# The sample block's state-space states: one product over 128 tokens per four sequences, for pairs of 32-row strips

## The chip, the core and the metric

The kernel runs on one core of one Trainium2 chip. The metric is device microseconds (us) of one execution of the whole program; the time of a version is the median of its runs. The engines are named as the profile names them: PE (TensorE matmuls) and PEld (its weight loads), DVE (VectorE), ACT (ScalarE), POOL (GpSimd) and SP (which issues the DMAs). PEclk is the clock that the throttle granted to TensorE, as a share of full speed.

## The reference, cut to what matters

One inference step of a layer: 1,024 prompt tokens of one new stream and 16 new tokens for each of 8 running streams (128 "sample" tokens) go through three token mixers side by side (stick-breaking attention, a Mamba-2 state-space group called SSD, forgetting attention called FoX), then a cross-attention and a feed-forward block. The change touches one product of the SSD group: the new state of each running stream.

```python
# sample group: b = 8 sequences, one chunk of 16 tokens each; 8 heads of 64 (p), state size 128 (n), 2 B/C groups
a_cum = jnp.cumsum(a, axis=2)
to_end = jnp.exp(a_cum[:, :, -1:, :] - a_cum)
chunk_states = jnp.einsum('bcshn,bcsh,bcshp->bchpn', B, to_end, x)   # sum over the 16 tokens s
chunk_decay = jnp.exp(a_cum[:, :, -1, :])
h_final = chunk_decay * h0 + chunk_states                             # output s_ssm, (8, 8, 64, 128)
```

## The kernel before, in words

All 1,152 tokens are nine blocks of 128; block 8 holds the sample tokens, sequence b in rows 16b to 16b+15. The first part of the program computes the input projections and, woven into one another by Python generators, three streams of work: the prompt attention (lines 560 to 606), the attention of the running streams over their caches (lines 863 to 959, cache rows loaded by SP at lines 882 and 942) and the SSD generator `ssd_gen` (lines 960 to 1200). The second part (output projection, cross-attention, feed-forward) is dense matmuls.

`ssd_gen` works through the blocks in the order 8, 0, 1, ..., 7. A block has the steps `load` (SP, lines 1037 to 1041), `prepare` (PE transposes at lines 1054 and 1058, POOL scalings through line 1030), `weights` (the masked decay matrix), `states`, `outputs` (eight products at line 1156) and `write`. A prompt block carries its state in `hT` (lines 1094 and 1100). Block 8 takes the `else` branch of `states`: the old states of four sequences lie in one SBUF tile of 128 x 3072 (`st8[hf]`, hf = 0 and 1, the first 2,048 columns), as 4 sequences b times 4 pairs of heads j times 128 states, with the pair's 2 x 64 channels on the partitions. For each half hf the branch

- transposes the old states (line 1129) and multiplies them with C for the token outputs: strips that are 32 columns of the array wide, accumulated in the PSUM tile `yo` (line 1132);
- makes the new states. `xe` holds x times its decay to the end of the chunk (128 tokens x 512 channels), `Bn` holds B (128 tokens x 2 groups x 128). A 32-row strip of tokens has two sequences. POOL first masks `Bn` by the parity of the sequence within its strip (line 1118, one 128 x 256 product for each of the two groups); a matmul over one strip (line 1139) then gives the states of its two sequences side by side in 256 columns. The two strips of a half go to two PSUM tiles, one of pool `psd` (2 buffers, one of them `yo` during this branch) and one of `pst` (3 buffers), and their matmuls are put to the scheduler as one group (`together`);
- decays and adds on DVE, one 128 x 128 operation for each sequence and pair of heads (line 1144), 32 in all, and stores the half (SP, line 1146).

Inputs of these matmuls are plain float32. The trace holds two matmul records for each of them and one for a transpose.

No order is written out by hand around this place. The kernel is recorded through a framework that sorts each engine's instructions at build time by a timeline of its own, with the priorities that the code gives (`hp`, `together`), and then inserts the waits. Every engine runs its list in that order. So a changed instruction can move others. Tiles of a pool are handed on when their last reader is done.

Of the kernel before, what the change touches and what calls it, by code (L numbers as in the profile page):

```python
# [12 lines left out]
ALU = mybir.AluOpType  # L13
# [4 lines left out]
P = 128  # L18
# [44 lines left out]
def tile_hybrid_step(ctx: ExitStack, tc: tile.TileContext, a: dict):  # L63
    nc = tc.nc
    ACT, DVE, POOL, PE, SP = nc.scalar, nc.vector, nc.gpsimd, nc.tensor, nc.sync
# [44 lines left out]
    def pd():  # L110
        return ps_t(psd, "d")
# [4 lines left out]
    def pT():  # L116
        return ps_t(pst, "t")
# [23 lines left out]
    rows = xc_t()  # L141
# [825 lines left out]
    def ssd_gen():  # L967
# [3 lines left out]
        bmask = sc[:, 1536:1544]  # L971
# [116 lines left out]
        def states(i, A, B, t1):  # L1088
            xT, br, zt, Bn, cb, xn, xd, xe, xD = views(A, B)
            hs = slice(8 * i, 8 * i + 8)  # L1090
            if i < 8:
                ps = pd()
                for g in range(2):
                    PE.matmul(ps[:, g * 256:(g + 1) * 256], xT[:, 6 + g, :], hT[:, g * 256:(g + 1) * 256],
                              start=True, stop=True)
                DVE.tensor_tensor(out=h3(t1), in0=h3(ps), in1=bc(ea[:, hs]), op=ALU.mult)
                heads_tt(hT, hT, dec[:, hs])
                ps = pd()
                for g in range(2):
                    PE.matmul(ps[:, g * 256:(g + 1) * 256], Bn[:, g * P:(g + 1) * P], xe[:, g * 256:(g + 1) * 256],  # L1100
                              start=True, stop=True)
                DVE.tensor_tensor(out=hT, in0=hT, in1=ps, op=ALU.add)
            else:
                hs_, cps = [], []
                for g, t in enumerate(st8):
                    hst = t[:, :2048].rearrange("p (u n) -> p u n", n=P)

                    cp = t[:, 2048:2304]
                    POOL.memset(cp, 0.0)
                    cv = bass.AP(cp.tensor, cp.offset, [list(cp.ap[0]), [64, 4], [48, 2], [1, 16]])  # L1110
                    POOL.tensor_copy(cv, xT[:, 6 + g, :].rearrange("p (i e t) -> p i e t", e=2, t=DEC_S))
                    hs_.append(hst.rearrange("p (b j) n -> p b j n", j=4))
                    cps.append(cp)
                yo = pd()
                bms = []
                for g in range(2):
                    bm = (A, B)[g][:, 2560:2816]
                    POOL.tensor_tensor(out=bm.rearrange("p (e n) -> p e n", n=P),
                                       in0=Bn[:, g * P:(g + 1) * P].unsqueeze(1).to_broadcast([P, 2, P]),
                                       in1=maskh.unsqueeze(2).to_broadcast([P, 2, P]), op=ALU.mult)  # L1120
                    bms.append(bm)
                for hf in range(2):
                    hst = hs_[hf]
                    for e in range(2):
                        h0 = []
                        for b in (e, 2 + e):
                            tp = pT()
                            for j in range(4):
                                PE.transpose(tp[:, j * P:(j + 1) * P], hst[:, b, j, :], ident)
                            h0.append(sg_t())  # L1130
                            ACT.copy(h0[-1], tp)
                        together([lambda r=32 * (2 * hf + x), g=g, x=x: PE.matmul(
                            yo[r:r + 32, g * 256:(g + 1) * 256], cps[g][:, 2 * r + 32 * e:2 * r + 32 * e + 32],
                            h0[x][:, g * 256:(g + 1) * 256], start=e == 0 and g == 0, stop=e == 1, skip_group_check=True)
                            for g in range(2) for x in (1, 0)])
                        yield
                    for j in range(4):
                        pss_ = [pd(), pT()]
                        together([lambda r=32 * (2 * hf + x), x=x: PE.matmul(
                            pss_[x][:, :256], xe[r:r + 32, j * P:(j + 1) * P], bms[j // 2][r:r + 32, :],  # L1140
                            start=True, stop=True) for x in range(2)])
                        for b in range(4):
                            bb = 4 * hf + b
                            DVE.scalar_tensor_tensor(hst[:, b, j, :], hst[:, b, j, :], dcol[:, 8 * j + bb:8 * j + bb + 1],
                                                     pss_[b // 2][:, b % 2 * P:(b % 2 + 1) * P], ALU.mult, ALU.add)
                    SP.dma_start(out=a["s_ssm"][0, 4 * hf:4 * hf + 4].rearrange("b h p n -> (b h p) n")
                                 .rearrange("(u p) n -> p u n", p=P), in_=hst.rearrange("p b j n -> p (b j) n"))
                    yield
                DVE.tensor_tensor(out=h3(t1), in0=h3(yo), in1=bc(ea[:, hs]), op=ALU.mult)
            pool_tt(t1, t1, xD, ALU.add)  # L1150
# [915 lines left out]
```

## Time and profile before

| | us |
|---|---|
| Median of 3 runs | 1885.78 |
| Lowest and highest of them | 1882.77, 1887.08 |
| The profiled execution's own time | 1894.55 |
| Its span in the trace | 1892.8 |

Positions are given in us from the start of the profiled execution's span. The branch for block 8 lies at 537.6 to 573.3 in it (first transpose of line 1129, last operation of line 1144). The mean granted TensorE clock over the span is 0.988.

### The profile page before, as it was taken

The numbers are of one execution on the slowest core, as the hardware profiler recorded it, in microseconds if no ns is written. First come the engines' busy times: TensorE is split into PE (matmuls) and PEld (weight loads), VectorE is DVE, ScalarE is ACT, GpSimd is POOL, SyncE is SP. The second block draws the span as 40 slices with busy tenths as digits, with TensorE's granted clock in tenths as the row PEclk, the third lists the DMA queues.
The fourth block names the chain that finished last, engine by engine and source line by source line (L and its number), as shares of the span: only waits on it lengthen the run. The fifth ranks groups of instructions, "written<-read, shape, count | busy, mean of one in ns | idle before, by whom it ended". The sixth has DMA issues, their size and how long they took to land.

```text
span 1892.8 us, 32368 instructions
## 1 busy us (share of the span) xinstructions
PE 1837.7 (97%) x12136; PEld 1638.6 (87%) x12136; DVE 886.4 (47%) x1798; ACT 802.1 (42%) x1719; POOL 617.9 (33%) x921
## 2 busy tenths in 40 slices
PE   7999999999999989999999989999999999999998
PEld 5899778888967767899988889999999999888886
DVE  3412323475656863444444586333333333455554
ACT  6522544545455862344332374333333333344443
POOL 7622425445115673111112107444444542000000
PEclk9999999999989999999999999999999999999999
DMA  9465654437587883245576124233322223657572
GB/s 338 145 189 149 206 142 133 147 109 207 179 249 228 282 290 102 108 134 173 173 271 219 56 81 112 75 87 79 76 71 70 70 70 105 207 187 243 174 243 89
DMA packets 291068, 296.64 MB, mean 157 GB/s; under 512 B 80092, under 2 KB 242884, under 8 KB 290912
## 3 DMA queue, kind: packets, MB, share of 16 engines
q1 hardware_dynamic: 290912, 294.57, 49.6%
q8 instruction: 96, 1.57, 0.3%
q14 instruction: 60, 0.49, 0.1%
HBM read 225.12 MB, written 69.91 MB: 156 GB/s over the span
## 4 chain that ended last, share of the span: by engine, by line
PE 83%; DMA 5%; DVE 4%; POOL 3%; ACT 3%; issue 2%; SPq 0%; DVEq 0%; POOLq 0%; ACTq 0%
PE psd L1868 11%; PE psd L328 10%; PE psd L329 10%; PE psd L330 10%; PE pst L1868 8%; PE pss L1868 4%; PE pss L328 3%; PE pss L330 3%; PE pss L329 3%; PE pso L1868 2%; POOL wl L132 2%; PE pst L328 1%; PE pst L329 1%; PE pst L330 1%; PE pso L593 1%
## 5 line engine op out<-in xcount | busy, mean ns | idle before, releaser
L132 POOL TENSOR_TENSOR wl<-wr,wh 128x256 fp32r<-128x256 f32 (+2 forms) x184 | 142.1, 805 | 233.0 <-ACT wh L292 232.8
L328 PE MATMUL psd<-act,wh 128*128 128x384 f32 x528 | 182.3, 345 | 0.0
L330 PE MATMUL psd<-act,wl 128*128 128x384 f32 x528 | 181.1, 343 | 0.6 <-POOL wl L132 0.6
L329 PE MATMUL psd<-act,wh 128*128 128x384 f32 x528 | 181.7, 344 | 0.0
L1868 PE MATMUL pst<-bT,tr 128*128 128x256 f32 (+1 forms) x1068 | 155.0, 293 | 0.0
L1868 PEld LDWEIGHTS pst<-bT,tr 128*128 128x128 f32 x1068 | 144.9, 188 | 0.1
L330 PE MATMUL psd<-wh,act 128*128 128x512 f32 (+3 forms) x424 | 136.9, 324 | 0.0
L329 PE MATMUL psd<-wl,act 128*128 128x256 f32 (+3 forms) x414 | 134.2, 325 | 2.7 <-POOL wl L132 2.7
L328 PE MATMUL psd<-wh,act 128*128 128x256 f32 (+3 forms) x414 | 133.3, 326 | 1.4 <-DMA act<-osc 1.0
L1868 PE MATMUL psd<-bT,tr 128*128 128x320 f32 (+1 forms) x912 | 132.8, 295 | 0.7 <-POOL tr L132 0.7
L1868 PEld LDWEIGHTS psd<-bT,tr 128*128 128x128 f32 x912 | 124.7, 188 | 1.0 <-POOL tr L132 0.9
L132 POOL TENSOR_TENSOR tr<-u,tr 128x256 fp32r<-128x256 f32 x110 | 82.6, 779 | 101.7 <-ACT tr L1704 83.8
L253 POOL TENSOR_SCALAR sm<-sm 128x1 f32<-128x1 f32 (+2 forms) x27 | 9.1, 338 | 297.3 <-ACT y L1970 207.8
L1843 DVE TENSOR_TENSOR tr<-tr,pst 128x256 f32<-128x256 f32 (+1 forms) x86 | 38.6, 449 | 139.9 <-ACT tr L1840 106.6
L330 PEld LDWEIGHTS psd<-act,wl 128*128 128x128 f32 x528 | 99.2, 188 | 3.2 <-issue 1.9
L132 POOL TENSOR_TENSOR ws<-ws 128x256 f32<-128x256 f32 (+2 forms) x100 | 69.3, 721 | 98.1 <-DVE ws L522 83.9
L328 PEld LDWEIGHTS psd<-act,wh 128*128 128x128 f32 x528 | 99.4, 188 | 2.2 <-issue 1.8
L329 PEld LDWEIGHTS psd<-act,wh 128*128 128x128 f32 x528 | 99.3, 188 | 1.9 <-issue 1.5
L132 POOL TENSOR_TENSOR tr<-raw,tr 128x256 fp32r<-128x256 f32 x94 | 69.2, 765 | 83.9 <-ACT tr L1704 75.7
L1704 ACT CAST tr<-tr 128x384 fp32r<-128x384 f32 (+1 forms) x70 | 37.6, 538 | 123.0 <-DMA tr<-hidsc 117.3
L329 PEld LDWEIGHTS psd<-wl,act 128*128 128x128 f32 x414 | 79.2, 191 | 10.9 <-POOL wl L132 4.0
L292 ACT CAST wh<-wr 128x512 fp32r<-128x512 f32 (+2 forms) x90 | 52.5, 622 | 81.7 <-PE psd L330 32.0
(643 smaller groups left out, 4730.5 us busy)
## 6 DMA issues: line engine op xcount, KB each, us to landing
u<-w_down SPq DMA_DIRECT2D x40, 512.0 KB
raw<-w_down SPq DMA_DIRECT2D x26, 512.0 KB
st<-qksc SPq DMA_DIRECT2D x48, 256.0 KB
wr<-w_in SPq DMA_DIRECT2D x44, 256.0 KB
tr<-hidsc SPq DMA_DIRECT2D x57, 192.0 KB
hidsc<-tr SPq DMA_DIRECT2D x34, 288.0 KB
qksc<-sg SPq DMA_DIRECT2D x48, 192.0 KB
wr<-cache_sb_k SPq DMA_DIRECT2D x32, 256.0 KB
```

What stands on the lines that cost most here:

```text
L132: POOL.tensor_tensor(out=out[:, a0:a1], in0=in0[:, a0:a1], in1=in1[:, a0:a1], op=op)
L253: POOL.tensor_scalar(v, ss, inv, EPS, ALU.mult, ALU.add)
L292: ACT.copy(hi, raw)
L328: PE.matmul(out, ah, bh, start=start, stop=False)
L329: PE.matmul(out, ah, bl, start=False, stop=False)
L330: PE.matmul(out, al, bh, start=False, stop=stop)
L593: return PE.matmul(po[r:r + 64, q_], vt[:, 2 * (k0 + i) + j, :], pfs[i][:, sl], start=start and k0 == 0 and (j == 0 or qp > 0), stop=k0 + ...
L1704: ACT.copy(hi, src)
L1843: DVE.tensor_tensor(out=at(out, g), in0=at(x, g), in1=ps[g][:, :GW[g]], op=op)
L1868: PE.matmul(dst[g][:, :GW[g]], x[:, ka], y[:, k, :], start=start and k == 0 and m == 0, stop=stop and k == 3 and m == 2, skip_group_check= ...
```

## The change

For each half, POOL now masks `Bn` with `bmask`, the one-hot map from token to sequence, into four blocks of 128 columns: tokens of other sequences become zeros. One matmul over all 128 tokens then gives the states of the four sequences of a half, for one pair of heads, in 512 columns. There are 8 such matmuls in place of 16 strips, 4 POOL products of 128 x 512 in place of 2 of 128 x 256, and one PSUM tile for each matmul, by turns of `psd` and `pst`. The masked rows lie in free columns of the same SBUF tiles (A, B and the two of `st8`). The DVE operations, the transposes and the stores are the same. Line numbers after this place are smaller by one.

```diff
-                bms = []
-                for g in range(2):
-                    bm = (A, B)[g][:, 2560:2816]
-                    POOL.tensor_tensor(out=bm.rearrange("p (e n) -> p e n", n=P),
-                                       in0=Bn[:, g * P:(g + 1) * P].unsqueeze(1).to_broadcast([P, 2, P]),
-                                       in1=maskh.unsqueeze(2).to_broadcast([P, 2, P]), op=ALU.mult)
-                    bms.append(bm)
+                rows = [[], []]
+                for hf in range(2):
+                    for g, t in enumerate((A, B)):
+                        bm = (t, st8[g])[hf][:, (2560, 2304)[hf]:(3072, 2816)[hf]]
+                        POOL.tensor_tensor(out=bm.rearrange("p (b n) -> p b n", n=P),
+                                           in0=Bn[:, g * P:(g + 1) * P].unsqueeze(1).to_broadcast([P, 4, P]),
+                                           in1=bmask[:, 4 * hf:4 * hf + 4].unsqueeze(2).to_broadcast([P, 4, P]), op=ALU.mult)
+                        rows[hf].append(bm)
...
                     for j in range(4):
-                        pss_ = [pd(), pT()]
-                        together([lambda r=32 * (2 * hf + x), x=x: PE.matmul(
-                            pss_[x][:, :256], xe[r:r + 32, j * P:(j + 1) * P], bms[j // 2][r:r + 32, :],
-                            start=True, stop=True) for x in range(2)])
+                        ps = (pd, pT)[j % 2]()
+                        PE.matmul(ps, xe[:, j * P:(j + 1) * P], rows[hf][j // 2], start=True, stop=True)
                         for b in range(4):
                             bb = 4 * hf + b
                             DVE.scalar_tensor_tensor(hst[:, b, j, :], hst[:, b, j, :], dcol[:, 8 * j + bb:8 * j + bb + 1],
-                                                     pss_[b // 2][:, b % 2 * P:(b % 2 + 1) * P], ALU.mult, ALU.add)
+                                                     ps[:, b * P:(b + 1) * P], ALU.mult, ALU.add)
```

How the order moves is shown at three places. The first is PE's list where the first strip stood (L1139; the new product is L1140, the C products L1132 become L1133, L924 are transposes of the cache attention).

```order
-L1132 MATMUL psd<-sg,act 32x256 x4
-L924 MATMUL pst<-ident,ws 128x128 x4
-L1139 MATMUL psd<-act 128x256
-L924 MATMUL pst<-ident,ws 128x128 x4
-L1132 MATMUL psd<-sg,act 32x256 x4
+L1133 MATMUL psd<-sg,act 32x256 x4
+L924 MATMUL pst<-ident,ws 128x128 x8
+L1140 MATMUL psd<-act 128x512
+L1133 MATMUL psd<-sg,act 32x256 x4
```

The new product stands behind all eight transposes, between the same two groups of C products.

The second place is PE's list in the second half of the branch. Before (L1129 are transposes of old states, L578 and L593 belong to the prompt attention, L1054 opens the next block):

```order
L1129 MATMUL pst<-ident,act 128x128 x12
L1139 MATMUL psd<-act 128x256
L1132 MATMUL psd<-sg,act 32x256 x4
L578 MATMUL pst<-ident,ws 128x128 x3
L1139 MATMUL pst<-act 128x256
L1139 MATMUL psd<-act 128x256
L1132 MATMUL psd<-sg,act 32x256 x4
L1139 MATMUL pst<-act 128x256
L593 MATMUL pso<-pt,st 64x256
L593 MATMUL pso<-pt,st 64x128
```

And now:

```order
L1130 MATMUL pst<-ident,act 128x128 x12
L1140 MATMUL psd<-act 128x512
L1133 MATMUL psd<-sg,act 32x256 x4
L578 MATMUL pst<-ident,ws 128x128 x3
L1140 MATMUL pst<-act 128x512
L1133 MATMUL psd<-sg,act 32x256 x4
L1140 MATMUL pst<-act 128x512
L593 MATMUL pso<-pt,st 64x256
L593 MATMUL pso<-pt,st 64x128
L578 MATMUL pst<-ident,ws 128x128 x4
```

The three strips that followed L593 in the list before are gone, and a whole product stands between the two groups of C products. From here to the end of the mixers (about 712 us in the trace) the lists of all engines differ in their order; in front of this place and behind 712 us they hold the same work in the same order.

The third place is POOL's list (L132 and L1030 are POOL's other products around it).

```order
 L1030 TENSOR_TENSOR act<-act,hb 128x256 x2
 L1030 TENSOR_TENSOR act<-act 128x256 x2
-L1118 TENSOR_TENSOR act<-act,maskh 128x256 x2
-L132 TENSOR_TENSOR sg<-sg,act 128x256 x2
...
+L1119 TENSOR_TENSOR act<-act 128x512 x4
+L132 TENSOR_TENSOR sg<-sg,act 128x256 x2
```

The four larger masks stand together where the two stood.

## The prediction

> **What bounds the kernel now.** I read the page first: busy shares, the slices, the chain that ended last.
>
> ```profile
> PE 1837.7 (97%) x12136; PEld 1638.6 (87%) x12136; DVE 886.4 (47%) x1798; ACT 802.1 (42%) x1719; POOL 617.9 (33%) x921
> PEclk9999999999989999999999999999999999999999
> PE 83%; DMA 5%; DVE 4%; POOL 3%; ACT 3%; issue 2%; SPq 0%; DVEq 0%; POOLq 0%; ACTq 0%
> ```
>
> PE is busy for 97% of the span and holds 83% of the chain, so time is saved where PE has less to do or does it faster. One slice of the clock, the twelfth (520 to 568 us), is below 9 tenths, and the branch for the sample block lies at 537.6 to 573.3. So the second view is the table of stretches of 4 us there. Its columns are PE, PEld, DVE, ACT and POOL busy, the granted clock, DMA share, GB/s.
>
> ```profile
> 548.00:552.00 4.00, 3.90 (x80) 2.90 (x79) 3.25 (x13) 1.80 (x5) 0.00 (x0) 1.00 0.00 0
> 552.00:556.00 4.00, 4.00 (x21) 2.73 (x20) 3.96 (x16) 0.00 (x0) 0.00 (x0) 1.00 0.89 298
> 556.00:560.00 4.00, 4.00 (x16) 2.93 (x15) 2.66 (x14) 3.15 (x8) 0.00 (x0) 0.51 0.81 196
> 560.00:564.00 4.00, 4.00 (x17) 2.05 (x15) 1.50 (x4) 2.01 (x4) 0.00 (x0) 0.50 1.08 308
> 564.00:568.00 4.00, 4.00 (x17) 1.56 (x15) 2.28 (x8) 1.81 (x3) 0.00 (x0) 0.50 0.43 138
> 568.00:572.00 4.00, 4.00 (x13) 2.27 (x12) 1.58 (x5) 1.10 (x2) 1.40 (x2) 0.50 0.77 250
> 572.00:576.00 4.00, 4.00 (x19) 3.35 (x17) 2.46 (x8) 2.14 (x6) 1.35 (x3) 0.50 0.37 114
> 576.00:580.00 4.00, 4.00 (x33) 3.31 (x32) 0.69 (x1) 1.49 (x4) 2.83 (x6) 0.93 0.82 238
> ```
>
> From 556 to 576 us TensorE has half its clock, although PE is busy in every one of these 20 us. The chain shows what it works on, and at what pace (start, length, work):
>
> ```profile
> 550.99 0.62 PE psd L1139 x2
> ...
> 552.90 0.62 PE pst L1139 x2
> 553.53 0.22 PE psd L1139
> 553.74 0.22 PE pst L1139
> 553.96 0.04 PE psd L1139
> ...
> 554.67 1.05 PE pst L1139 x4
> ...
> 557.50 1.15 PE psd L1139 x2
> 558.65 2.75 PE pst L1129 x12
> ...
> 562.55 1.85 PE psd L1132 x8
> ...
> 565.23 0.72 PE pst L1139
> 565.96 0.01 PE psd L1139
> 565.96 0.42 PE pst L1139
> 566.38 0.01 PE psd L1139
> ...
> 572.86 1.05 PE psd L1054 x4
> 573.91 1.49 PE pst L578 x7
> ```
>
> A lone strip (two records) takes 0.62 us at full clock and 1.15 at half. In front of the drop, 552 to 556 holds five strips with 0.62 + 0.22 + 0.22 + 0.04 + 1.05 = 2.15 us, over half of PE's time there. During the drop PE alternates between strips, C products (L1132, 32 columns of the array) and short runs of transposes. The clock comes back after a stretch, 572.86 to 575.4, with no strip and no C product in it. My reading, which the trace suggests and doesn't show: matmuls that use a part of the array count as little activity, and enough of them close together drop the clock. The stretch then holds itself down, since at half clock each of them lasts longer.
>
> **The products themselves.** The group line of the chain between 530 and 580 us puts L1139 at 12.3% + 6.4% of 50 us, and one row elsewhere prices a float32 matmul over all 128 rows:
>
> ```profile
> by line: PE pst L1139 12.3%; PE pso L593 10.4%; PE pst L578 8.8%; DMA act<-acsc 7.8%; PE psd L1132 7.4%; PE pst L1129 7.2%; PE psd L1139 6.4%; DMA acsc<-so 5.9%; PE pso L933 4.3%; PE psd L1156 3.5%; PE pss L560 3.4%; PE psd L1054 3.0%; PE p
> 643.07 0.87 PE psd L1094 x4
> ```
>
> 18.7% of 50 us is 9.35 us; two earlier strips off the chain, at 0.62 each, make it 10.6 us for all 16. The eight behind 556 us have 6.6 of it (three lone ones at 1.15, the first of them at 557.50, two that ran side by side from 565.23 in 1.16, and three at the end in 2.0); at full clock they would be 3.3. So at one clock the strips cost 4.0 + 3.3 = 7.3 us. L1094 is two matmuls of 256 columns in 0.87 us, which is one of 512; eight new products are 7.0 us. **Term 1: -0.3 us.** A quarter of the rows did not make a strip cheaper: a lone strip's 0.62 us is even more than the 0.435 us of 256 columns over all rows.
>
> The Trainium skill, "TensorE: Matmul & The Clock Gate", Part 3 (packing small matmuls), speaks against the change: matmuls on different row strips run concurrently in the array, so a pair would cost about as much as one of them. The trace agrees for the pairs that start together (two strips in 1.16 us at half clock, against 1.15 for one) but most strips here run alone; by that rule alone the sum would be +2.3 us, the third rival below.
>
> **The clock.** Five stretches of 4 us lose 0.49 + 4 x 0.50 of their clock, and 576 to 580 loses 0.07: 4 x 2.56 = 10.2 us of full clock. In the changed order the partial matmuls left are the four groups of C products, about 1 us each, and a whole product stands between them each time (two places of the order). So I take it that the clock stays up in this stretch. What is late then is DVE, which has the same 32 operations:
>
> ```profile
> 545.00:555.00 10.00, 9.90 (x113) 6.84 (x113) 8.45 (x33) 4.77 (x12) 0.00 (x0) 1.00 0.47 138
> 555.00:565.00 10.00, 10.00 (x38) 6.08 (x36) 5.31 (x21) 5.16 (x11) 0.00 (x0) 0.55 0.97 276
> 565.00:575.00 10.00, 10.00 (x37) 5.68 (x36) 6.17 (x20) 4.11 (x8) 1.75 (x3) 0.50 0.43 134
> ```
>
> DVE works 8.45 + 5.31 + 6.17 = 19.9 us of these 30. With 10.2 us less there would be 19.8, all of it DVE's. At the best share it reaches here, 0.845, its work takes 23.6 us, so the clock is worth between 30 - 23.6 = 6.4 and 10.2 us. I take 7.7, nearer to the lower end, because 552 to 556 (DVE 3.96 of 4) shows it full already with PE at full clock. **Term 2: -7.7 us.**
>
> The Trainium skill, same page, Part 1, has the clock fall to half when the array is idle for a window of about 3.4 us, and advises against idle gaps longer than that. No gap of PE stands ahead of this drop (4.00 of 4 us busy), so the trace shows a drop that this advice would not explain; by it the strips are not the cause and the sum is term 1 alone, -0.3 us, the first rival below.
>
> **POOL.** Two masks become four of twice the columns:
>
> ```profile
> 541.48 1.30 POOL L1118 TENSOR_TENSOR act<-act,maskh 128x256 f32<-128x256 f32 x2
> 569.18 1.40 POOL L132 TENSOR_TENSOR sg<-sg,act 128x256 f32<-128x256 f32 x2 [26.41 <-issue]
> ```
>
> Two took 1.30 us; four of double size are 5.2, so they end at 546.7 where they ended at 542.8. The 26.4 us of idle time behind them cover it, even if they took three times as long. The first whole product needs only the first mask (542.8), and its place in the list is behind L1132 and eight transposes, about 545. Nothing is paid. The new product waits for one PSUM tile where two strips waited for two; DVE's reading of it is the same work, and I cost it at nothing inside term 2.
>
> **What lies behind.** Up to 712 us the mixers are short chains over all engines, in a new order, with a load on the chain here and there:
>
> ```profile
> 581.91 5.60 DMA act<-acsc
> 584.00:588.00 4.00, 2.61 (x21) 1.49 (x22) 1.08 (x3) 1.89 (x6) 3.14 (x7) 1.00 1.02 315
> 588.00:592.00 4.00, 2.82 (x23) 2.34 (x22) 3.96 (x10) 1.79 (x6) 2.71 (x5) 1.00 1.04 412
> ```
>
> These loads are issued when SP's list gets there, which follows the chain, so I let the gain pass through. The new order I cost at 0, between -3 and +3 us: one stall like this one (1.39 + 1.18 = 2.6 us of PE idle) less or more.
>
> **The sum.** -0.3 - 7.7 = -8.0 us. The profiled execution took 1894.55 us, which makes 1886.5 of it; it lies 8.8 us above the median of the runs, 1885.78. Applied to the median, the forecast is 1877.8 us, with a range of its own from 1885.8 - 10.5 - 3 = 1872.3 to 1885.8 - 6.7 + 3 = 1882.1.
>
> **Rivals.**
>
> 1. The clock drops anyway, or dropped only in the profiled execution. For: the C products are as partial as before, and the 8.8 us by which that execution was slower are nearly the 10.2 of the drop. Against: the same list of instructions runs each time, and nothing in it depends on profiling. Then only term 1 is left, 1885.5 us, with the order's 3 us to either side.
> 2. Slower: DMA takes the gain and the clock falls somewhere else. Place: the cache loads of 584 to 592, where DMA is at 1.02 and 1.04 and PE already idles 2.6 us. If the loads come no earlier than now, the 8 us come back as idle time of PE, and what idle time does to the clock stands elsewhere in this trace:
>
> ```profile
> 280.00:284.00 4.00, 2.57 (x17) 1.43 (x15) 1.27 (x1) 2.89 (x7) 2.83 (x5) 1.00 0.76 213
> 284.00:288.00 4.00, 3.02 (x15) 1.67 (x16) 3.90 (x7) 3.95 (x10) 4.00 (x4) 0.80 1.05 272
> 288.00:292.00 4.00, 3.90 (x19) 3.35 (x20) 3.12 (x5) 1.89 (x4) 4.00 (x6) 0.50 1.16 317
> 292.00:296.00 4.00, 4.00 (x31) 4.00 (x30) 1.29 (x3) 0.56 (x2) 4.00 (x8) 0.84 0.19 41
> ```
>
>  With 1.4 and 1.0 us idle of 4 the clock fell, for a loss of 4 x (0.20 + 0.50 + 0.16) = 3.4 us: 1889.2 us. It decides if the cache loads land no earlier than they do now. Against it: between 556 and 576 DMA is at 0.81, 1.08, 0.43, 0.77 and 0.37, so there is room to move them forward.
> 3. Slower: the concurrency that is given up. If all strips had run in pairs of 1.16 us at half clock, 0.58 at full, eight pairs would be 4.6 us against 7.0, +2.3 us and 1888.1 with the clock as it is. Only some did; the 10.6 us measured speak against it.
>
> That the change does not do what it says is ruled out by the order: 8 products of 512 columns stand for 16 strips.
>
> **Chances.** The forecast 0.62, rival 1 0.20, rival 2 0.11, rival 3 0.04; 0.03 for what I don't see. A measurement of this kernel can tell about 0.2%, 3.8 us, from no change. The forecast is faster but for its upper edge (0.58 of 0.62, the other 0.04 same); rival 1 is faster by luck of the order in a quarter of its cases (0.05), same in half (0.10), slower in the rest (0.05); rival 2, at +3.4 us and the order's 3, is slower in 0.08 and same in 0.03; rival 3 is same in 0.03 and slower in 0.01; the 0.03 unseen go one to each. Together: faster 0.64, same 0.21, slower 0.15. The range from 1872 to 1889 holds the forecast's own, rivals 1 and 3, and most of rival 2.
>
> **What would show it.** In the profile after: eight groups of L1140 of 0.87 us on PE; PEclk at 1.00 from 548 to 580; the last DVE update of the branch (573.3 now) between 563 and 567; DVE near full in the stretch; the dense part behind 712 us unchanged, only earlier. Term 2 is wrong if a stretch of 0.50 stands there again, or if PE is idle there for DVE by more than 4 us. Pass-through is wrong if the branch ends earlier and the first product of the output projection does not.

## The result, and the profile after

The changed kernel takes 1899.28 us (median of 7 runs, 1890.94 to 1902.02) where the kernel before takes 1887.08 beside it (7 runs, 1882.77 to 1891.18). The ratio is 1.0051, with a 95% interval from 1.0034 to 1.0068: slower by half a per cent, where 1877.8 us was forecast. The ratio, here and below, is not simply the quotient of the two medians (1.0065 here). Measured a second time, beside the experiments, it took 1899.09 us, ratio 1.0058 [1.0040, 1.0076]. Its profiled execution took 1896.22 us, with a span of 1894.5 us and a mean granted clock of 0.989. In the changed kernel the lines of the code behind the branch are one lower than before (L1168 is before's L1169, L1320 is L1321).

The page of the changed kernel, for the lines read before: PE is as busy as it was, the slice of the clock with the branch has recovered, and DMA holds 8% of the chain where it held 5%.

```profile
PE 1833.2 (97%) x12120; PEld 1634.0 (86%) x12120; DVE 895.5 (47%) x1798; ACT 801.8 (42%) x1719; POOL 618.2 (33%) x923
PEclk9999998999999999999999999999999999999999
PE 81%; DMA 8%; DVE 4%; POOL 3%; ACT 2%; issue 2%; SPq 1%; DVEq 0%; POOLq 0%; ACTq 0%
```

The table of stretches of 4 us round the branch, with the columns of the prediction (PE, PEld, DVE, ACT, POOL, the granted clock, DMA share, GB/s):

```profile
552.00:556.00 4.00, 4.00 (x17) 2.39 (x16) 3.13 (x12) 0.98 (x2) 0.00 (x0) 1.00 0.71 214
556.00:560.00 4.00, 1.97 (x16) 1.51 (x13) 3.19 (x15) 2.15 (x6) 0.00 (x0) 1.00 0.87 256
560.00:564.00 4.00, 3.42 (x10) 1.29 (x12) 1.67 (x6) 2.82 (x6) 0.00 (x0) 0.63 1.14 324
564.00:568.00 4.00, 4.00 (x21) 1.44 (x17) 2.91 (x10) 1.81 (x3) 0.00 (x0) 0.94 0.63 142
568.00:572.00 4.00, 4.00 (x33) 3.50 (x32) 1.75 (x7) 2.71 (x7) 2.60 (x5) 1.00 0.66 173
```

The 20 us at half clock are gone. In their place PE is idle for 2.03 of the 4 us from 556, and the clock falls behind that, by 0.37 + 0.06 of 4 us = 1.7 us. The last state update begins at 569.4 us where it began at 573.3, and the first transpose of the branch at 536.3 where it was at 537.6. The first add of the output projection stands at 711.6, where it stood at 711.5. So the branch ends 4 us earlier (2.6 us of that is its own length, the rest came from ahead of it), and the 140 us behind it have used that up. Behind this point the two traces stay close: from that add to the start of the last operation of line 1840 (1839 now) it is 892.0 us, and 893.0 before. From there to the end of the span the changed kernel takes 2.6 us more.

The chain that ended last between 540 and 720 us, by line, shows what came in (its end is cut off in the view). The first fence is the kernel before, the second the changed one:

```profile
by line: DMA act<-acsc 11.1%; issue 6.4%; PE pst L578 3.5%; ACT ws L542 3.5%; PE pst L1139 3.4%; PE pso L593 3.4%; PE pso L933 3.1%; PE psd L1156 3.1%; DMA act<-mixsc 3.0%; POOL act L1030 2.9%; DVE ws L535 2.8%; ACT act L1077 2.5%; ACT act 
```

```profile
by line: DMA act<-acsc 16.2%; DMA wr<-cache_fox_k 7.5%; issue 4.3%; PE pso L593 4.2%; DMA act<-mixsc 4.0%; PE pst L888 3.3%; ACT ws L542 3.3%; DVE ws L535 2.9%; PE pst L578 2.7%; DVE act L1085 2.5%; PE psd L1094 2.3%; DMA mixsc<-so 2.2%; AC
```

Loads of the blocks' decay rows (acsc) and of cached keys (cache_fox_k) hold 23.7% of these 180 us, 43 us, where before only the former has a part in the chain, with 20. PE's waits from 535 to 715 us name the instructions (engine, tile and line, what it waited for: us in total, times, longest):

```profile
PE pst L888 <- DMA wr<-cache_fox_k: 5.2, 3, 2.3
PE psd L1167 <- DVE st L1320: 3.0, 1, 3.0
PE pst L1130 <- ACT sg L1132: 2.4, 1, 2.4
```

These are three kinds of place: the transposes of cached keys, in three groups, wait for their loads; the output projection waits for DVE's adds; the branch's own transposes wait for ACT. Together 10.6 us. The experiments ask which of them is the cost, and what became of the clock.

### The profile page after: what moved, and what is told of

The parts are those of the page before. It is cut to its first block, busy times and chain, and to the rows that moved or that the text cites. A ratio compares the mean times of both kernels' runs of the same rounds, so it can differ in the third digit from the quotient of the medians.

```text
span 1894.5 us, 32317 instructions
## 1 busy us (share of the span) xinstructions
PE 1833.2 (97%) x12120; PEld 1634.0 (86%) x12120; DVE 895.5 (47%) x1798; ACT 801.8 (42%) x1719; POOL 618.2 (33%) x923
## 4 chain that ended last, share of the span: by engine, by line
PE 81%; DMA 8%; DVE 4%; POOL 3%; ACT 2%; issue 2%; SPq 1%; DVEq 0%; POOLq 0%; ACTq 0%
PE psd L1867 11%; PE psd L328 10%; PE psd L329 10%; PE psd L330 10%; PE pst L1867 8%; PE pss L1867 4%; PE pss L328 3%; PE pss L329 3%; PE pss L330 3%; PE pso L1867 2%; DMA act<-acsc 2%; PE pso L593 2%; PE pst L328 1%; PE pst L329 1%; PE pst L330 1%
## 5 line engine op out<-in xcount | busy, mean ns | idle before, releaser
L132 POOL TENSOR_TENSOR wl<-wr,wh 128x256 fp32r<-128x256 f32 (+2 forms) x184 | 141.0, 800 | 232.9 <-ACT wh L292 190.1
L328 PE MATMUL psd<-act,wh 128*128 128x384 f32 x528 | 182.3, 346 | 0.2 <-ACT wh L292 0.2
L328 PE MATMUL psd<-wh,act 128*128 128x256 f32 (+3 forms) x414 | 133.5, 326 | 0.8 <-DMA act<-osc 0.4
L132 POOL TENSOR_TENSOR tr<-u,tr 128x256 fp32r<-128x256 f32 x110 | 82.7, 780 | 100.2 <-ACT tr L1703 82.3
L328 PEld LDWEIGHTS psd<-act,wh 128*128 128x128 f32 x528 | 99.4, 188 | 2.7 <-issue 1.6
L132 POOL TENSOR_TENSOR ws<-ws 128x256 f32<-128x256 f32 (+2 forms) x100 | 69.0, 717 | 99.3 <-DVE ws L522 91.0
L132 POOL TENSOR_TENSOR tr<-raw,tr 128x256 fp32r<-128x256 f32 x94 | 69.2, 765 | 84.5 <-ACT tr L1703 76.4
L328 PEld LDWEIGHTS psd<-wh,act 128*128 128x128 f32 x414 | 79.8, 193 | 8.6 <-issue 1.1
## 6 DMA issues: line engine op xcount, KB each, us to landing
hidsc<-tr SPq DMA_DIRECT2D x34, 288.0 KB
```

Source lines behind the costliest of these rows:

```text
L132: POOL.tensor_tensor(out=out[:, a0:a1], in0=in0[:, a0:a1], in1=in1[:, a0:a1], op=op)
L328: PE.matmul(out, ah, bh, start=start, stop=False)
```

## The experiments

Theory A, mine at the start: the half clock comes from matmuls over part of the array, whole products cure it in every execution, and the new order behind the branch costs more than that. (A strip here is a matmul over 32 rows of the array, a whole product one of 512 columns over all 128.) Theory B, a rival: the half clock was an accident of one trace, and the products cost the same. Theory C, another: whole products are themselves slower here, since PE waits for DVE at them.

Most kernels below differ in the order of the engines' lists alone. Each list is given in full, as numbers in the order of recording, and each row is tied to the one ahead of it. The lists themselves are left out of the cuts below, and comments in them are notes for the reader:

```diff
+        for p, q in zip(order, order[1:]):
+            tc.add_manual_dep(ins[q], ins[p].name, info, reason="pinned")
```

All medians, with the ratio to the kernel before in runs beside it (the median of all 122 of those is 1888.4 us). The last column is the time in the one trace of each from the branch's first transpose to the first add of the output projection:

| Kernel | median us | ratio [95%] | branch to add, us |
|---|---|---|---|
| before against itself | 1889.21 | 1.0004 [0.9991, 1.0017] | 174.5 |
| before, one ACT copy ahead | 1886.63 | 1.0001 [0.9986, 1.0016] | 166.0 |
| strips' matmuls over all rows, old order | 1888.41 | 0.9999 [0.9985, 1.0014] | 167.9 |
| new products, old order | 1890.18 | 1.0007 [0.9995, 1.0018] | 168.5 |
| the same, ACT's copies first | 1889.57 | 1.0000 [0.9986, 1.0014] | 167.7 |
| new order in the branch only | 1890.91 | 1.0011 [0.9997, 1.0026] | 167.3 |
| new order up to the second key group | 1891.49 | 1.0020 [1.0009, 1.0032] | 169.9 |
| new order behind the branch | 1895.05 | 1.0035 [1.0021, 1.0049] | 173.8 |
| new order from the second key group | 1898.76 | 1.0047 [1.0028, 1.0067] | 176.8 |
| the changed kernel | 1899.09 | 1.0058 [1.0040, 1.0076] | 173.3 |
| with ACT's copies first | 1894.39 | 1.0037 [1.0022, 1.0052] | 171.9 |
| with DVE's adds first | 1893.77 | 1.0033 [1.0020, 1.0047] | 171.3 |
| with SP's key loads first | 1899.57 | 1.0064 [1.0046, 1.0081] | 176.2 |
| with all three | 1896.17 | 1.0044 [1.0027, 1.0061] | 175.0 |
| with ACT's copies and DVE's adds first | 1893.17 | 1.0021 [1.0006, 1.0035] | 168.1 |

### Is it the products or the order?

**The new products in the old order.** The changed code, with all lists as in the kernel before; a product stands where the strip into its PSUM pool stood, and its four updates where the first pair of them stood.

```diff
         tile_hybrid_step(tc, aps)
+        pinned(tc)    # PINS: the lists of the kernel before
```

> The changed kernel with every engine's list pinned to the order of the kernel before; each product stands where the strip of its PSUM pool stood, its four DVE updates together. Theory A: no drop of the clock, and nothing lost behind the branch: 1879 to 1883 us, 4 to 8 faster than before. Theory B: 1885 to 1889, the products cost the same. Theory C: about 1897, as the changed kernel.

Measured: 1890.18 us, ratio 1.0007 [0.9995, 1.0018]. PE's longest waits in its trace, from 535 to 708 us:

```profile
PE psd L1094 <- ACT sg L1168: 2.6, 1, 2.6
PE psd L1054 <- DMA act<-xbcsc: 2.0, 2, 1.3
PE pso L933 <- ACT act L925: 1.4, 1, 1.4
PE psd L1167 <- DVE st L1320: 1.3, 1, 1.3
PE pst L888 <- DMA wr<-cache_fox_k: 0.6, 1, 0.6
```

The waits for cached keys are 0.6 us where the changed kernel has 5.2, and the output projection waits 1.3 where it has 3.0. So in the mixers the products cost nothing that can be told: the interval goes from -0.9 to +3.4 us. The interval of the changed kernel lies above it, so at least most of the slowdown is the order's: 1899.09 - 1890.18 = 8.9 us. Theory C, with 1897 us for this run, falls. The gain that theory A wanted is not there either; in this, theory B is right.

One thing does come with the products, far behind the branch. From the end of the last operation of line 1839 (1840 or 1841 in kernels with other line numbers) to the end of the program, the 14 traces with whole products take 288.4 to 290.6 us, the six other traces of this document 287.5 to 288.0. In this stretch PE waits once for a cast by ACT, at a product of L328 near 1630 us: 1.68 to 2.38 us in those 14 traces, 0.79 to 1.12 in the six. So some 0.7 us of the 1890.18 may be the products' own; why that wait grew, no run shows.

**Only the rows changed.** The old 16 matmuls of 256 columns in the old order, but each over all 128 rows, with the masked `Bn`.

```diff
-    pss_[x][:, :256], xe[r:r + 32, j * P:(j + 1) * P], bms[j // 2][r:r + 32, :],
+    pss_[x][:, :256], xe[:, j * P:(j + 1) * P], rows[hf][j // 2][:, 256 * x:256 * x + 256],
```

> The kernel before with its order pinned and its 16 strips kept as 16 matmuls of 256 columns at the same places, but each over all 128 rows, with B masked as in the changed kernel; only the rows of the array differ from before. Theory A: no drop of the clock, 1879 to 1883 us. If the number of rows has nothing to do with the clock: the drop stays, 1886 to 1889 us.

Measured: 1888.41 us, ratio 0.9999 [0.9985, 1.0014]. The four doubled masks of POOL cost nothing that can be told here either, and the 1879 to 1883 us of theory A did not come.

### Does the half clock come with the strips?

**The kernel before, three more traces; the changed kernel, one.**

The kernels are unedited.

> The kernel before, unchanged, for a second trace. Theory A (matmuls on a part of the array drop the clock in every execution, and the new order behind the branch is what costs time): a stretch at half clock of 12 to 20 us somewhere between 550 and 580 us again. Theory B (the drop was an accident of the first trace): no stretch, or one under 5 us. Time 1883 to 1891 us by both.

> The changed kernel, unchanged, for a second trace. Theory A: at most 4 us at half clock in the branch, its end some 5 us ahead of before; the lead is gone by 700 us, with PE idle and clock lost behind the branch. Theory C (the whole products themselves are slow, since PE waits for DVE between them): no lead at the end of the branch. Time 1891 to 1902 us by both.

> The kernel before once more. If the half clock comes with the strips each time, 10 to 20 us of it stand between 550 and 580 us again, and the time is 1893 to 1895. If it came by chance in the two traces seen, nothing of it, and 1887 to 1890.

> The kernel before against itself. Ratio 1.000 within 0.0015. If profiled executions of it are slower than the others (three of them took 1894.0 to 1894.6, the median of the others is 1888.2), its profiled run is again 1894, and its other runs are about 1888.

Measured: the three traces of before took 1894.0, 1894.5 and 1892.29 us, the changed kernel 1902.85. The last of the kernels before was also run against itself, 1889.21 us, ratio 1.0004 [0.9991, 1.0017]. Stretches of 8 us round the end of the branch, first the second, third and fourth trace of the kernel before, then the new products in the old order:

```profile
556.00:564.00 8.00, 8.00 (x33) 5.57 (x31) 6.25 (x25) 4.34 (x10) 0.00 (x0) 0.66 0.95 273
564.00:572.00 8.00, 8.00 (x38) 3.70 (x37) 4.16 (x14) 3.02 (x6) 0.33 (x1) 0.70 0.76 224
```

```profile
556.00:564.00 8.00, 8.00 (x71) 5.87 (x64) 5.89 (x25) 1.23 (x3) 0.00 (x0) 0.83 0.50 168
564.00:572.00 8.00, 7.27 (x47) 3.90 (x46) 5.80 (x22) 6.58 (x14) 0.00 (x0) 1.00 0.96 250
```

```profile
556.00:564.00 8.00, 6.94 (x30) 3.23 (x30) 3.25 (x12) 5.21 (x11) 0.00 (x0) 0.64 1.11 293
564.00:572.00 8.00, 8.00 (x28) 4.50 (x27) 5.49 (x18) 2.61 (x6) 1.41 (x2) 0.50 0.49 139
```

```profile
556.00:564.00 8.00, 7.02 (x39) 3.28 (x38) 7.05 (x25) 6.45 (x14) 0.18 (x1) 1.00 1.06 282
564.00:572.00 8.00, 8.00 (x63) 6.46 (x62) 4.74 (x15) 4.93 (x11) 6.51 (x10) 1.00 1.01 294
```

With strips the long half clock stands in three traces of four: the one of the prediction, the second and the fourth. The third lost 1.7 us of clock in all. A fifth trace with strips (the last experiment, below) has none. None of the 15 traces with products over all rows (14 with whole products, one of the run just above) has a loss of over 2 us there. So the strips seem to have a part in it, which is argued from these counts and not shown, and they don't bring it each time.

What it is worth in the metric is another matter. The four profiled executions of the kernel before took 1892.3 to 1894.6 us; of its 122 other runs in these experiments, 5 took 1894 or more. Those 122 have a mean granted clock of 0.991, the four profiled ones 0.988, 0.989, 0.988 and 0.991. A run's time goes with its clock: the 22 runs at 0.989 or less took 1892.4 us in the mean, the 19 at 0.993 or more 1885.5. So three of the four traces of this kernel had lost more clock than most runs. Beside these traces the new products in the old order save 2 to 6 us (168.5 us from the branch to the add, against 170.3 to 174.5), beside the fifth trace with strips nothing (166.0); in the medians they save nothing. Why the profiled executions of this one kernel lie so high stayed open: those of the other kernels lie on both sides of their medians.

### Which part of the order costs?

**Four cuts.** The changed code with the lists of one order up to a point and of the other behind it. The first pair is cut at the last state update of the branch, the second pair ahead of the second group of key transposes, at about 612 us.

```diff
+        pinned(tc)    # PINS: new order up to the cut, old order behind it (or the reverse)
```

> The changed code, every engine's list as in the changed kernel up to the last state update of the branch, and behind it in the order of the kernel before. Theory 1 (the cost lies in the lists behind the branch, where the transposes of the cached keys stand closer together and wait for their loads): about 1892 us, the old order's 1890.2 and up to 3 for the wait of 2.4 us at the branch's second half. Theory 2 (that wait and the clock that falls with it are the cost, carried on to the end): 1896 to 1899 us.

> The changed code, every list in the order of the kernel before up to the last state update of the branch, and behind it as in the changed kernel. Theory 1: 1896 to 1898 us, the old order's 1890.2 and the 5.2 us that PE idles for the loads of the cached keys, with some clock. Theory 2: 1890 us, and no idle time of PE for the loads of the cached keys beyond 1 us.

> The changed code in the order of the kernel before up to the second group of transposes of cached keys (about 612 us), and behind it in the order of the changed kernel. If the waits for loads in the second and third group (2.3 to 3.4 and 1.9 us) with the clock's fall behind them, and the 3.0 us for the last state updates at 711, are the cost: 1894 to 1896 us. If the first group (2 us of waits) and the mixers round it are: 1890 to 1892.

> The complement of the last cut: the changed code in the changed kernel's order up to the second group of transposes of cached keys, and in the old order behind it. If the cost lies behind that point: 1889 to 1892 us, ratio under 1.002. If it lies in the branch and the first group: 1896 or more.

Measured: in the branch only 1890.91 us, behind it 1895.05; up to the second group 1891.49, from it on 1898.76. The front part costs one to two per mille, the back part 3.5 to 4.7, and the sums of either pair (4.6 and 6.7 per mille) hold the 5.8 of the whole within their intervals, though each sum counts the products' 0.7 per mille twice. For the changed kernel run beside them, 1894 to 1896 us were expected if the first pair adds up and 1898 to 1900 if its parts make each other worse; it took 1899.09. The intervals are too wide to tell the two apart. PE's rows with the longest idle times in the trace of the new order from the second group on (start, length, line, operation; in brackets the idle time ahead and its cause):

```profile
624.31 1.10 PE L888 MATMUL pst<-ident,wr 128*128 128x128 f32 x4 [3.64 <-DMA wr<-cache_fox_k]
...
673.44 0.45 PE L888 MATMUL pst<-ident,wr 128*128 128x128 f32 x1 [3.27 <-DMA wr<-cache_fox_k]
...
717.17 1.12 PE L1167 MATMUL psd<-ident,sg 128*128 128x128 f32 x4 [4.83 <-DVE st L1320]
```

The three places of the changed kernel's trace behind 612 us stand here alone, with 11.7 us, and the clock falls at each of them, near the end of the idle time or right behind it: 0.57 at 624 to 628, 0.52 and 0.63 at 672 to 680, 0.57 at 716 to 720.

### Which rows?

**ACT: a copy behind a load.** In ACT's list the four copies of the second half's transposes stand behind three rows of the next block that wait for a load. Trace of the changed kernel:

```profile
557.85 0.98 ACT L1077 ACTIVATE act<-act 128x128 f32<-128x128 f32 x3 [4.87 <-DMA act<-acsc]
...
559.76 0.56 ACT L1132 COPY sg<-pst 128x512 f32<-128x512 f32 x1
```

PE had made the first three sets of them by 557.97 us and was idle until 560.38, for want of a free PSUM tile. In the first kernel the copies, with the softmax row L542 that stands among them, are moved ahead in the changed order, in the second in the old one.

```diff
 L542 ACTIVATE ws,sm<-ws,sm 128x768
+L542 ACTIVATE ws,sm<-ws,sm 128x896
+L1132 COPY sg<-pst 128x512 x4
 L1077 ACTIVATE act<-act 128x128 x3
-L542 ACTIVATE ws,sm<-ws,sm 128x896
-L1132 COPY sg<-pst 128x512
 L1082 ACTIVATE act<-act 128x384
-L1132 COPY sg<-pst 128x512 x2
 L1082 ACTIVATE act<-act 128x640
-L1132 COPY sg<-pst 128x512
```

> The changed kernel's own lists, but for nine rows of ACT's: the four copies of the second half's transposes (L1132) stand ahead of the three L1077 that wait for a load. Theory 1: PE's 2.4 us of idle time at 558 us is gone and the clock stays up there; the gain of up to 4 us goes in the waits for the loads behind, 1897 to 1899 us. Theory 2: 1890 to 1894 us.

> The changed code in the order of the kernel before, with the four copies of the second half's transposes ahead of the three L1077 in ACT's list. If that wait costs in the old order what it cost in the new one (4.9 us less with the copies first): 1886 to 1888 us, ratio below 0.9995. If other work of PE covers it there: 1890 us, as without.

Measured: 1894.39 us in the new order, 1889.57 in the old. In the new order PE's 2.41 us for ACT became 1.13 us for DVE, and the clock stayed up in the branch. The interval [1.0022, 1.0052] still overlaps that of the changed kernel [1.0040, 1.0076], so the 4.7 us of the medians are likely but not certain. In the old order the wait was 0.5 us to begin with, and the move is worth nothing that can be told.

**DVE: adds behind loads.** At the output projection the changed order has four splits of loaded rows (L1389) in one go, and the adds that free PE's PSUM tiles (L1320) behind them. The splits wait for ACT's casts of rows that are still being loaded:

```profile
707.72 1.99 DVE L1389 TENSOR_TENSOR act<-act 128x768 fp32r<-128x768 f32 x2 [0.29 <-ACT act L1388]
709.90 1.83 DVE L1389 TENSOR_TENSOR act<-act 128x768 fp32r<-128x768 f32 x2 [0.20 <-ACT act L1388]
711.65 0.68 DVE L1320 TENSOR_TENSOR st<-st,psd 128x512 f32<-128x512 f32 x1
```

PE had written the sums by 709.4 us. In the kernel before, three of the adds stand ahead of the last two splits and the fourth between them.

```diff
 L1371 TENSOR_TENSOR act<-act,ws 128x1024
-L1389 TENSOR_TENSOR act<-act 128x768 x4
+L1389 TENSOR_TENSOR act<-act 128x768 x2
 L1320 TENSOR_TENSOR st<-st,psd 128x512
 L1320 TENSOR_TENSOR st<-st,pss 128x512
 L1320 TENSOR_TENSOR st<-st,psd 128x512
 L1320 TENSOR_TENSOR st<-st,pss 128x512
+L1389 TENSOR_TENSOR act<-act 128x768 x2
```

> The changed kernel's own lists, but for four rows of DVE's: the four adds of the output projection (L1320) stand ahead of the last two L1389, as in the kernel before. If they wait there behind rows that wait for loads, PE's idle time at 711 us falls from 2.6 to 3.0 to about 1.3, and the time to 1896 to 1898. If the adds are late for another reason: 1899, idle time as it was.

Measured: 1893.77 us, ratio 1.0033 [1.0020, 1.0047]. PE's row there:

```profile
712.19 0.66 PE L1167 MATMUL psd<-ident,sg 128*128 128x128 f32 x4 [0.83 <-DVE st L1320]
```

The idle time fell from 3.01 us (2.55 and 2.56 in the other two traces) to 0.83. The medians fell by 5.3 us, more than this place explains; here too the intervals overlap, by 0.0007, so how much of it is the adds' is not shown.

**SP: key loads behind block loads.** SP's list has three large loads of the next block between the loads of cached keys:

```profile
615.56 0.54 SPq L882 DMA_DIRECT2D wr<-cache_fox_k  x1
616.15 0.45 SPq L1037 DMA_DIRECT2D act<-xbcsc  x1
616.65 0.57 SPq L1039 DMA_DIRECT2D act<-acsc  x1
617.26 0.43 SPq L1041 DMA_DIRECT2D act<-zsc  x1
617.79 1.47 SPq L882 DMA_DIRECT2D wr<-cache_fox_k  x3
```

```diff
-L882 DMA wr<-cache_fox_k 128x512
+L882 DMA wr<-cache_fox_k 128x512 x4
 L1037 DMA act<-xbcsc 128x8x128
 L1039 DMA act<-acsc 128x1024
 L1041 DMA act<-zsc 128x512
-L882 DMA wr<-cache_fox_k 128x512 x3
...
-L882 DMA wr<-cache_fox_k 128x512
+L882 DMA wr<-cache_fox_k 128x512 x2
 L1037 DMA act<-xbcsc 128x8x128
 L1039 DMA act<-acsc 128x1024
 L1041 DMA act<-zsc 128x512
-L882 DMA wr<-cache_fox_k 128x512
```

> The changed kernel's own lists, but for SP's in two places: the loads of cached keys stand ahead of the next block's three loads (L1037, L1039, L1041) in the second and in the third group. If PE's waits there (2.3 to 3.6 and 1.7 to 3.3 us) come from that place in SP's list: both under 1 us, and 1894 to 1896 where the changed kernel has 1899. If they come from the ring of four tiles alone: the waits stay and so does the time.

Measured: 1899.57 us, ratio 1.0064 [1.0046, 1.0081]. The waits for cached keys in these two groups are gone, as expected, and the time is not. PE's rows there, and DVE's:

```profile
627.80 0.79 PE L560 MATMUL pss<-st 128*128 128x512 f32 x1 [4.77 <-DVE sm L535]
...
677.08 1.22 PE L1069 MATMUL psd<-act 128*128 128x128 f32 x4 [3.39 <-ACT sg L1168]
```

```profile
626.14 1.07 DVE L1079 TENSOR_SCALAR act<-act 128x128 f32<-128x128 f32 x5 [4.87 <-DMA act<-acsc]
627.12 0.61 DVE L535 CUSTOM_DVE_ANT_0 ws<-pss,xc,sm 128x384 f32<-128x384 f32 x1
```

Now the decay rows come later, DVE's L1079 waits 4.87 us for them, and the softmax row L535, for which PE waits, stands behind it in DVE's list. The waits for cached keys, 2.28 and 1.86 us in the trace of the changed kernel, were changed for longer ones, 4.77 and 3.39.

**Together.** First all three moves; then ACT's and DVE's, with one more of the same kind: at 671 us ACT's copy L1168 ahead of three L1077 that wait for a load.

```diff
 L890 COPY kf<-pst 128x2x256 x2
+L1168 COPY sg<-psd 128x512
 L1077 ACTIVATE act<-act 128x128 x3
-L1168 COPY sg<-psd 128x512
 L1082 ACTIVATE act<-act 128x384
```

> The changed kernel's own lists with all three moves: ACT's copies ahead of the L1077, SP's loads of cached keys ahead of the block's, DVE's adds ahead of the last two L1389. If these three places are the cost: 1889 to 1892 us, as with the old order. If the new order costs in many small places: 1893 or more.

> The changed kernel's own lists with two moves that left PE no new wait, and a third of the same kind: DVE's adds (L1320) ahead of the last two L1389, ACT's four copies of the branch ahead of the L1077 that wait for a load, and at 671 us ACT's copy L1168 ahead of the three L1077 there. If such places, where a row that PE waits for stands behind one that waits for a load, are the cost of the new order: 1889 to 1891 us, since the first two took 5.3 and 4.7 us off by themselves. If they overlap: 1892 to 1894.

Measured: 1896.17 us with SP's move, 1893.17 without it, ratio 1.0021 [1.0006, 1.0035]. This interval lies below the changed kernel's: a few rows in two lists, taken together, give back 5.9 of the 10.7 us that the changed kernel lay above before beside it (1899.09 - 1893.17; 1899.09 - 1888.35). They do not add up to all of it (1889 to 1891 us was expected for that), and the waits for cached keys are still there (1.46 and 1.94 us):

```profile
618.84 0.66 PE L888 MATMUL pst<-ident,wr 128*128 128x128 f32 x4 [1.46 <-DMA wr<-cache_fox_k]
...
665.07 0.30 PE L888 MATMUL pst<-ident,wr 128*128 128x128 f32 x1 [1.94 <-DMA wr<-cache_fox_k]
```

**The same place in the kernel before.** Its ACT list has the copy L1169 behind three L1077 as well, and each of its four traces shows PE waiting 1.90 to 2.45 us for it. The kernel before, with the copy ahead and nothing else:

```diff
+L1169 COPY sg<-psd 128x512
 L1077 ACTIVATE act<-act 128x128 x3
-L1169 COPY sg<-psd 128x512
```

> The kernel before in its own order, but for one row of ACT's list: at 671 us the copy L1169, which stands behind three L1077 that wait 3.2 us for a load, ahead of them. PE waits 1.9 to 2.4 us for it in each trace of the kernel before. If such places decide: 1885 to 1887 us where the kernel before takes 1888.3, ratio 0.998 to 0.999. If the next wait takes it: 1888.

Measured: 1886.63 us, ratio 1.0001 [0.9986, 1.0016]. That wait is gone, and the next operations took part of it:

```profile
664.79 1.20 PE L578 MATMUL pst<-ident,ws 128*128 128x128 f32 x9 [1.63 <-DVE ws L547]
...
668.64 1.08 PE L593 MATMUL pso<-pt,st 128*64 128x256 f32 x8 [0.76 <-ACT pt L581]
```

This trace, with strips, has no half clock in the branch: 1.00 in every stretch from 548 to 580 us. From the branch's first transpose to the first product of line 1156 it takes 31.2 us, as long as the new products in the old order (31.3), where the three traces with the half clock took 38.9, 34.7 and 38.9, and the other one without it 34.4. No version here is faster than the kernel before by what can be measured.

## Why the prediction was wrong

**The products (term 1, -0.3 us): right.** Four records, two products, took 1.94 us in the changed kernel, and one took 0.86 us in its chain, for 0.87 forecast. In the old order they change the time by 0.7 per mille, and the interval holds nothing as well. One reading in this term was off: that a lone strip costs more than 256 columns over all rows. It compares a lone strip with one of two products in a row. In the run with only the rows changed, lone products of 256 columns over all rows take 0.59 to 0.70 us in the timeline, where a lone strip takes 0.69 at full clock.

```profile
553.62 1.94 PE L1140 MATMUL pst<-act 128*128 128x512 f32 x4
```

**POOL: right.** Four masks took 4.33 us, 5.2 forecast, and ended at 544.5; no other engine waited for them.

```profile
540.20 4.33 POOL L1119 TENSOR_TENSOR act<-act 128x512 f32<-128x512 f32 x4
```

**The clock (term 2, -7.7 us): the step "I take it that the clock stays up in this stretch" held in the trace, its worth in the metric failed.** The long half clock did go, though even in the trace it brought less than the 7.7 us: the last state update of the branch began at 569.4 us, not between 563 and 567, for PE now waited 2.41 us for ACT's copies there and the clock fell once more, for 1.7 us. (With the old order it began at 566.3.) But the long half clock is in three of five traces with strips, and none of the three kernels with products over all rows in the old order is faster than the kernel before (ratios 0.9999, 1.0000 and 1.0007). I argued that it must come each time, since "the same list of instructions runs each time". That does not follow: the list was the same in all five traces but for one row, and the clock was not. Rival 1 came nearer ("dropped only in the profiled execution"), though the drop came in some profiled executions and not in others, and its 1885.5 us missed the order's cost as the forecast did; 0.20 was too little. The 8.8 us by which the profiled execution lay above the median were the sign. A term that rests on one execution's clock is to be checked against the clock of the others.

**"I let the gain pass through" and "The new order I cost at 0, between -3 and +3 us: one stall like this one": this step failed.** It is what the prediction named as its test: the branch ended 4 us earlier, and the first add of the output projection did not. The new order cost 8.9 us, three times the end of my range. The stalls in the trace were not one but five, with 10.6 us: one for ACT's copies, one for DVE's adds, three for cached keys. The first two are of one kind: a row that PE waits for stands, in the list of an engine that works in order, behind a row that waits for a load. Curing both, and a third of that kind, brought the time down by 5.9 us; the waits for cached keys were not cured by a move in SP's list. I had weighed the order by the work in it, which is the same, and not by what stands behind what. A difference of the lists of ACT, DVE and SP between 612 and 712 us would have shown two of these places ahead of any run; the prediction read the order at the branch only.

**Rival 2 was near.** Its mechanism was that the cache loads take the gain and the clock falls behind PE's idle time. In the trace of the changed kernel it does, at 560, 580 and 624 us. But it was placed at the first group of cache loads (584 to 592), while most of the cost lies behind 612, and at 3.4 us where it was 9. **Rival 3** (strips side by side) cannot be told apart by the times: its +2.3 us lies within the -0.9 to +3.4 us of the new products in the old order. The traces speak against it, since most strips ran alone; and it is far from the 12 us that the changed kernel lost.

What stays open: the last 3 us or so of the order's cost (1893.17 against 1890.18 us), since curing the key loads by SP's list alone moved the wait elsewhere; what the products do to the wait near 1630 us; and why strips lose the clock in some executions and not in others.

## What to carry to other kernels

Where a scheduler sorts the lists, a change of a few instructions is a change of the order of some hundreds, and that can cost more than the instructions. So pin the old order and run the new instructions in it: that parts the two effects in one run. Compare the lists for rows that wait for a load and for what stands behind them, and move single rows; but expect that a load that is brought forward pushes back another, as SP's did here. And a cost that is read from one profiled execution is to be looked for in the medians before it is counted.

## What the runs showed of the hardware

- In the branch and right behind it, TensorE's clock fell to half for 10.2, 17.1 and 20.5 us, with PE busy in almost every one of them, in three of five traces with 32-row strips, and in none of 15 with products over all rows. All 40 falls between 510 and 730 us in the 20 traces last 3.41 us (29 of them) or 2, 3, 5 or 6 times as long. It also fell behind idle times of PE: 2.41 us of idle time, then 0.63 and 0.94 in the next two stretches of 4 us. Not each such idle time did it: behind the 3.01 us at 712 the clock stayed at 1.00 in the same trace.
- It can last without strips: in one trace (new order in the branch only) PE was idle for 1.95 us at 523 and then had half its clock for 10.2 us, with ordinary work:

```profile
524.00:532.00 8.00, 6.73 (x37) 6.76 (x38) 0.47 (x2) 0.81 (x2) 0.89 (x3) 0.65 1.01 331
532.00:540.00 8.00, 8.00 (x51) 4.67 (x50) 1.38 (x6) 3.38 (x9) 0.00 (x0) 0.71 1.05 345
```

- Most falls behind idle times cost 1.7 us of clock, as (0.37 + 0.06) x 4 at 560 us and (0.31 + 0.11) x 4 at 580. The Trainium skill, "TensorE: Matmul & The Clock Gate", Part 1 (The HAM clock gate), has the clock at half until a window of about 3.4 us was busy, which is the same 1.7 us; the single falls agree with that. The long stretches do not: there PE was busy at half clock for three to six times 3.41 us. The same part has it fall when the array was idle for such a window: here it fell behind 1.95 and 2.41 us of idle time, and it fell into the long stretches with the strips with no idle time of PE in the 7 us ahead of two of them and 1.03 us ahead of the third, so there the runs disagree. Nor is idle time of that size enough: in the fifth trace with strips PE was idle for 1.03 us at 558 and the clock stayed up.
